# Sample states of a hybrid decoder step: loaded four ahead instead of two, decayed in place by ScalarE, first group one down tile later

## The chip, the cores and the metric

The kernel runs on one core of a Trainium2 chip. The metric is the device time of one execution in microseconds (us), the median of several runs. The engines are TensorE (PE in the profile; PEld is its weight load), VectorE (DVE), ScalarE (ACT), GpSimd (POOL) and SyncE (SP). SP and POOL here mostly issue DMAs; the DMAs of both run on the core's 16 DMA engines.

## The reference, cut to what matters

One inference step of a one-layer decoder, for 512 tokens of a new sequence and 8 sample rows of one token each (520 columns in all): a half-step SwiGLU FFN, a mixer (causal pooling beside a Mamba-2 style SSD), a second half-step FFN, a final norm. The part that the change touches is the new recurrent state of the 8 sample rows, one of the outputs. For a sequence of one token the scan of the reference shrinks to

```
h = a[..., None, None] * h + s      # a = exp(dt * A), s = (dt * x) outer B
```

for 16 heads of 64 x 128 numbers in each of 8 rows. The kernel keeps it as 8 blocks of 128 x 128 for each row: 64 blocks in all. Nothing else reads these new states; they only go to the output. The FFN beside it is

```
def _swiglu(x, wg, wu, wd):
    return (jax.nn.silu(x @ wg) * (x @ wu)) @ wd
```

with a model width of 1024 and an FFN width of 2816, that is 22 feature tiles of 128.

## The kernel before, in words

Every fp32 product is made of three matmuls on a high and a low part: `mm3` (L116 to L119) multiplies high by high (L117), high by low (L118) and low by high (L119). So each weight unit of 128 x 1024 numbers goes through three steps: SP loads it into half of a `raw` pair (a pair holds two units, and there are two pairs), ACT casts it to the high part `whi` (L107), and DVE subtracts that to get the low part `wlo` (L108). There are three buffers for `whi` and three for `wlo`.

An FFN (`class Ffn`) works in chunks of 8, 8 and 6 feature tiles (`rest`, L307). In a chunk it computes gate and up projections (banks `A` and `BE` of PSUM, weights from `w2gu` in the second FFN), and then, in `down` (L339), multiplies the chunk's features `g` with eight down units d = 0 to 7, each 48 matmuls into a bank `dn`. For each d, `done` (L353) takes the bank out: `td` (L356) on DVE, and an add into the residual `h` (L360). `load` (L247) brings in the next gate and up pair; DVE's `s` adds (L258 to L260) read it, and its SP loads (L251, L252) can only start when a `raw` pair is free, that is when DVE has made both low parts of the two down units that sat in it.

The new sample states run inside the second FFN, in the down stages of the first two chunks. `new_states` (L795) is a generator with 16 groups (8 rows by 2 halves); `STATES` (L37) says how many groups are begun ahead of each down unit d, and L376 and L377 advance it. One group is: a load of a broadcast row `br` (64 KB) and of the state `hs` (256 KB), both issued from POOL (L798, L800); four ACT instructions that make an outer product `so` from `br` and the column `sxdt` (L814); four DVE instructions that compute state times decay plus `so` in place (L816); and a store of `hs` from POOL to `out_nss` (L818). The loads of group i + 2 are issued in group i. There are three `br` and three `hs` buffers and two of `so`, so that the load of a new `hs` waits until the store of the group three before it has landed, and POOL's queue stands still behind that wait. The first two groups are loaded long before, when the second FFN begins (L500).

What sets the order: a scheduler orders each engine's instructions by a simulated timeline, apart from those marked to stay in program order among themselves (all of the states' instructions). So a group may end up ahead of or behind a cast, and the order on an engine is fixed when the kernel is built.

Of the kernel before, what the change touches and what calls it, by code (L numbers as in the profile page):

```python
# [9 lines left out]
F32 = mybir.dt.float32  # L10
F32R = mybir.dt.float32r
AF = mybir.ActivationFunctionType
ALU = mybir.AluOpType
# [3 lines left out]
P = 128  # L17
# [16 lines left out]
CHUNKS = (8, 8, 6)  # L34
NG = 9
ON_ACT = 4
STATES = (0, 1, 1, 1, 2, 1, 1, 1)  # L37

CONV_PLAN = (
    "b0 b1 d0 b2 b3 x0 x1 v0 d1 x2 x3 d2 X0 p0 y0 c0 A0 p1 x4 m0 x5 B0 c1 p2 m1 A1 x6 c2 p3 A2 B1 x7 "  # L40
# [22 lines left out]
def tile_trunk_step(ctx: ExitStack, tc: tile.TileContext, ins: dict, outs: dict):  # L63
# [132 lines left out]
    class Ffn:  # L196
# [142 lines left out]
        def down(self, c, lo, hi, after):  # L339
# [35 lines left out]
            for d in range(first, KD):  # L375
                for _ in range(STATES[d] if self.states is not None else 0):  # L376
                    next(self.states)  # L377
# [172 lines left out]
def mixer(tc, ins, outs, e):  # L550
    nc = tc.nc
# [189 lines left out]
    sdec = cst.tile([P, NX, NS], F32, tag="sdec", name="sdec")  # L741
    sxdt = cst.tile([P, NX, NS], F32, tag="sxdt", name="sxdt")
# [5 lines left out]
    def rows_bc(b, a, g):  # L748
        return scr_bc.rearrange("b (a g n) -> b a g n", a=2, g=2)[b, a, g].unsqueeze(0).to_broadcast([P, P])
# [44 lines left out]

    def new_states(wx):  # L795
        def load(b, g):
            br = wx.tile([P, P], F32, tag="sb", bufs=3, name=f"br{b}{g}")
            tc.keep_in_program_order(nc.gpsimd.dma_start(out=br, in_=rows_bc(b, 0, g)))  # L798
            hs = wx.tile([P, 4, P], F32, tag="sh", bufs=3, name=f"hs{b}{g}")
            tc.keep_in_program_order(nc.gpsimd.dma_start(out=hs, in_=ins["state_ssm"][:, b, 4 * g : 4 * g + 4]))  # L800
            return br, hs

        todo = [(b, g) for g in range(2) for b in range(NS)]
        ahead = [load(*todo[0]), load(*todo[1])]
        for i, (b, g) in enumerate(todo):
            yield
            br, hs = ahead.pop(0)
            if i + 2 < len(todo):
                ahead.append(load(*todo[i + 2]))
            o = wx.tile([P, 4, P], F32, tag="so", bufs=2, name=f"so{b}{g}")  # L810
            for q in range(4):
                j = 4 * g + q
                tc.keep_in_program_order(
                    nc.scalar.activation(out=o[:, q], in_=br, func=AF.Copy, scale=sxdt[:, j, b : b + 1]))  # L814
                tc.keep_in_program_order(
                    nc.vector.scalar_tensor_tensor(out=hs[:, q], in0=hs[:, q], scalar=sdec[:, j, b : b + 1],  # L816
                                                   in1=o[:, q], op0=ALU.mult, op1=ALU.add))
            tc.keep_in_program_order(nc.gpsimd.dma_start(out=outs["nss"][:, b, 4 * g : 4 * g + 4], in_=hs))  # L818
        yield

# [268 lines left out]
```

## Time and profile before

| | us |
|---|---|
| time before, median of 3 runs | 1012.86 (1012.05 to 1013.91) |
| the profiled execution, own time | 1014.71 |
| its span | 1012.8 |
| PE busy in the span | 977.1 (96%) |
| DVE, ACT, POOL busy | 807.1, 526.1, 85.9 |
| granted TensorE clock, mean | 0.993 |

The profiled execution lies 1.85 us above the median of the runs, and 1.9 us of its time lie around the span. A line of the timeline or of the windows gives times from the start of the span. In the line of a group or a timeline, the square bracket is the idle time of the engine just before the instruction, and what ended it. The two down stages in question lie at about 730 to 784 us and 860 to 917 us of the span; the first FFN has two down stages of the same work without the states, at 109 to 161 us and 238 to 290 us.

### The profile page before, as it was taken

The numbers are of one execution on the slowest core, as the hardware profiler recorded it, in microseconds if no ns is written. First come the engines' busy times: TensorE is split into PE (matmuls) and PEld (weight loads), VectorE is DVE, ScalarE is ACT, GpSimd is POOL, SyncE is SP. The second block draws the span as 40 slices with busy tenths as digits, with TensorE's granted clock in tenths as the row PEclk, the third lists the DMA queues.
The fourth block names the chain that finished last, engine by engine and source line by source line (L and its number), as shares of the span: only waits on it lengthen the run. The fifth ranks groups of instructions, "written<-read, shape, count | busy, mean of one in ns | idle before, by whom it ended". The sixth has DMA issues, their size and how long they took to land.

```text
span 1012.8 us, 19354 instructions
## 1 busy us (share of the span) xinstructions
PE 977.1 (96%) x7850; PEld 953.8 (94%) x7850; DVE 807.1 (80%) x1408; ACT 526.1 (52%) x877; POOL 85.9 (8%) x157
## 2 busy tenths in 40 slices
PE   7999999999999999999999999999999999999994
PEld 6999999999999999999899989899999999989994
DVE  7999556995569688788979987999847999467866
ACT  7566324664146455685855235666633666434552
POOL 0000000000000000157311000100013000120000
PEclk9999999999999999999999999999999999999997
DMA  6333222332223233363244421332345423453203
GB/s 193 109 125 126 84 84 94 117 105 97 92 84 105 86 105 111 103 200 116 90 144 125 141 84 43 122 126 87 122 137 184 135 108 111 103 188 123 94 32 84
DMA packets 44072, 114.44 MB, mean 113 GB/s; under 512 B 6408, under 2 KB 15560, under 8 KB 43984
## 3 DMA queue, kind: packets, MB, share of 16 engines
q1 hardware_dynamic: 40912, 103.78, 30.0%
q0 software_dynamic: 3072, 9.44, 3.8%
q8 instruction: 61, 1.00, 0.4%
q14 instruction: 27, 0.22, 0.1%
HBM read 105.86 MB, written 7.34 MB: 112 GB/s over the span
## 4 chain that ended last, share of the span: by engine, by line
PE 84%; DVE 8%; ACT 3%; DMA 2%; issue 1%; POOL 0%; SPq 0%; DVEq 0%; ACTq 0%
PE A L117 8%; PE A L118 7%; PE A L119 7%; PE dn L119 6%; PE dn L117 6%; PE BE L117 6%; PE BE L119 6%; PE dn L118 6%; PE BE L118 6%; PE P L230 2%; PE wo L117 2%; PE wo L118 2%; PE wo L119 2%; PE inz L117 2%; DMA raw<-in_w2gu 2%; PE inz L119 2%
## 5 line engine op out<-in xcount | busy, mean ns | idle before, releaser
L117 PE MATMUL dn<-g,whi_1d 128*128 128x260 f32 x352 | 99.5, 283 | 1.8 <-ACT whi_1d L107 1.6
L356 DVE SCALAR_TENSOR_TENSOR td<-dn,r_f 128x520 f32<-128x520 f32 x40 | 27.8, 698 | 90.8 <-PE dn L119 90.8
L118 PE MATMUL dn<-g,whi_1d 128*128 128x260 f32 x352 | 99.4, 283 | 0.0
L119 PE MATMUL dn<-g,wlo_1d 128*128 128x260 f32 x352 | 99.1, 283 | 0.0
L119 PE MATMUL dn<-g,wlo_2d 128*128 128x260 f32 x256 | 73.6, 288 | 3.7 <-DVE wlo_2d L108 3.7
L117 PE MATMUL dn<-g,whi_2d 128*128 128x260 f32 x256 | 73.1, 286 | 0.4 <-ACT whi_2d L107 0.4
L118 PE MATMUL dn<-g,whi_2d 128*128 128x260 f32 x256 | 73.0, 285 | 0.0
L117 PEld LDWEIGHTS dn<-g,whi_1d 128*128 128x128 f32 x352 | 66.2, 188 | 2.4 <-ACT whi_1d L107 2.0
L118 PEld LDWEIGHTS dn<-g,whi_1d 128*128 128x128 f32 x352 | 66.3, 188 | 0.0
L119 PEld LDWEIGHTS dn<-g,wlo_1d 128*128 128x128 f32 x352 | 66.1, 188 | 0.0
L286 ACT COPY ac<-A 128x260 f32<-128x260 f32 x123 | 45.8, 373 | 35.8 <-PE A L119 34.3
L107 ACT CAST whi_1d<-raw_1d 128x1024 fp32r<-128x1024 f32 (+1 forms) x24 | 23.4, 979 | 70.8 <-PE dn L118 62.3
L258 DVE TENSOR_TENSOR s<-raw 128x1024 f32<-128x1024 f32 x41 | 49.9, 1218 | 7.4 <-DMA raw<-in_w2gu 7.4
L119 PEld LDWEIGHTS dn<-g,wlo_2d 128*128 128x128 f32 x256 | 48.9, 191 | 4.6 <-DVE wlo_2d L108 4.6
L230 PE MATMUL P<-xg_f,raw 128*128 128x260 f32 x192 | 45.3, 393 | 5.8 <-DMA raw<-in_w1gu 5.3
L117 PEld LDWEIGHTS dn<-g,whi_2d 128*128 128x128 f32 x256 | 49.1, 192 | 0.6 <-ACT whi_2d L107 0.6
L118 PEld LDWEIGHTS dn<-g,whi_2d 128*128 128x128 f32 x256 | 49.0, 191 | 0.0
L230 PEld LDWEIGHTS P<-xg_f,raw 128*128 128x128 f32 x192 | 37.0, 196 | 11.7 <-ACT xg_f L179 5.3
L118 PE MATMUL wo<-catg,whi_wo 128*128 128x260 f32 x128 | 36.4, 285 | 1.3 <-DVE catg L946 1.3
L117 PE MATMUL wo<-catg,whi_wo 128*128 128x260 f32 x128 | 37.3, 292 | 0.3 <-DVE h L915 0.3
L117 PE MATMUL inz<-xh_mx,whi_inz 128*128 128x260 f32 x128 | 36.8, 287 | 0.0
L117 PE MATMUL inx<-xh_mx,whi_inx 128*128 128x260 f32 x128 | 36.4, 285 | 0.0
(1339 smaller groups left out, 3918.2 us busy)
## 6 DMA issues: line engine op xcount, KB each, us to landing
raw<-in_w2gu SPq DMA_DIRECT2D x44, 512.0 KB, 4.4
raw<-in_w1gu SPq DMA_DIRECT2D x42, 512.0 KB, 4.4
raw_1d<-in_w1d SPq DMA_DIRECT2D x16, 512.0 KB, 4.4
raw_2d<-in_w2d SPq DMA_DIRECT2D x16, 512.0 KB, 4.7
raw_wo<-in_w_out SPq DMA_DIRECT2D x12, 512.0 KB, 4.5
ab<-scr_acs SPq DMA_DIRECT2D x8, 512.0 KB, 4.6
h<-in_state_ssm SPq DMA_DIRECT2D x16, 256.0 KB, 4.4
raw_inz<-in_w_in SPq DMA_DIRECT2D x8, 512.0 KB, 3.9
```

Of the source, the lines that this page charges most:

```text
L107: nc.scalar.copy(h, src)
L117: nc.tensor.matmul(ps, whi, xhi, start=start, stop=False, **kw)
L118: nc.tensor.matmul(ps, whi, xlo, start=False, stop=False, **kw)
L119: nc.tensor.matmul(ps, wlo, xhi, start=False, stop=stop, **kw)
L230: nc.tensor.matmul(self.banks[f, u][b][:, :HB], ws(self.raw[f][:, u], j + 4 * q), xg[:, slot[q]], start=j == q == 0, stop=j == 3 and q == ...
L258: nc.vector.tensor_tensor(out=s1, in0=diag, in1=up0, op=ALU.add)
L286: nc.scalar.copy(keep, out[:, :HB])
L356: nc.vector.scalar_tensor_tensor(out=t, in0=banks[d][:, :, :HB], scalar=-0.5, in1=self.nx[3].rearrange("p (b t) -> p b t", b=2), op0=ALU.mult,
```

## The change

Three things change. Loads: the first four groups are loaded ahead, and group i issues the loads of group i + 4; `br` and `hs` have five buffers each. Arithmetic: ACT now multiplies the state block by its decay in place (the four ACT instructions read and write `hs`), and DVE adds `br` times `sxdt` to it; the tile `so` is gone. Place: in each of the two chunks no group is begun ahead of d = 0 or d = 1, and two groups are begun at d = 3 and at d = 5, where before one was begun at d = 1, 2, 3, 5, 6 and 7 and two at d = 4.

```diff
-STATES = (0, 1, 1, 1, 2, 1, 1, 1)
+STATES = (0, 0, 1, 2, 1, 2, 1, 1)
...
         def load(b, g):
-            br = wx.tile([P, P], F32, tag="sb", bufs=3, name=f"br{b}{g}")
+            br = wx.tile([P, P], F32, tag="sb", bufs=5, name=f"br{b}{g}")
             tc.keep_in_program_order(nc.gpsimd.dma_start(out=br, in_=rows_bc(b, 0, g)))
-            hs = wx.tile([P, 4, P], F32, tag="sh", bufs=3, name=f"hs{b}{g}")
+            hs = wx.tile([P, 4, P], F32, tag="sh", bufs=5, name=f"hs{b}{g}")
             tc.keep_in_program_order(nc.gpsimd.dma_start(out=hs, in_=ins["state_ssm"][:, b, 4 * g : 4 * g + 4]))
             return br, hs
 
         todo = [(b, g) for g in range(2) for b in range(NS)]
-        ahead = [load(*todo[0]), load(*todo[1])]
+        ahead = [load(*t) for t in todo[:4]]
         for i, (b, g) in enumerate(todo):
             yield
             br, hs = ahead.pop(0)
-            if i + 2 < len(todo):
-                ahead.append(load(*todo[i + 2]))
-            o = wx.tile([P, 4, P], F32, tag="so", bufs=2, name=f"so{b}{g}")
+            if i + 4 < len(todo):
+                ahead.append(load(*todo[i + 4]))
             for q in range(4):
                 j = 4 * g + q
                 tc.keep_in_program_order(
-                    nc.scalar.activation(out=o[:, q], in_=br, func=AF.Copy, scale=sxdt[:, j, b : b + 1]))
+                    nc.scalar.activation(out=hs[:, q], in_=hs[:, q], func=AF.Copy, scale=sdec[:, j, b : b + 1]))
                 tc.keep_in_program_order(
-                    nc.vector.scalar_tensor_tensor(out=hs[:, q], in0=hs[:, q], scalar=sdec[:, j, b : b + 1],
-                                                   in1=o[:, q], op0=ALU.mult, op1=ALU.add))
+                    nc.vector.scalar_tensor_tensor(out=hs[:, q], in0=br, scalar=sxdt[:, j, b : b + 1], in1=hs[:, q],
+                                                   op0=ALU.mult, op1=ALU.add))
             tc.keep_in_program_order(nc.gpsimd.dma_start(out=outs["nss"][:, b, 4 * g : 4 * g + 4], in_=hs))
```

## The prediction

> **What bounds the kernel now.** I read the page's first part: PE is busy 96% of the span, so a change to work on ACT, DVE and POOL can only pay where PE stands still for that work. Then the waits of PE in the two down stages of the second FFN, where all the states are computed, then the timelines there, and last the first FFN's down stages, which do the same matmuls without states. The windows view of the four down stages, each from the cast of unit d = 0 to the start of `td` of d = 7 (columns: window, length, busy time of PE, PEld, DVE, ACT, POOL, clock, DMA share, GB/s):
>
> ```profile
> 109.22:161.12 51.90, 50.90 (x423) 50.48 (x422) 23.80 (x29) 10.84 (x13) 0.00 (x0) 1.00 0.27 95
> 237.77:289.92 52.15, 51.15 (x423) 50.73 (x422) 23.79 (x29) 10.84 (x13) 0.00 (x0) 1.00 0.26 93
> 730.12:783.63 53.51, 51.39 (x423) 50.77 (x422) 32.10 (x62) 20.47 (x45) 10.75 (x20) 1.00 0.54 162
> 860.24:916.87 56.63, 53.08 (x423) 52.24 (x422) 32.08 (x62) 20.37 (x45) 9.70 (x18) 0.97 0.50 152
> ```
>
> The states make the stages 53.51 - 51.90 = 1.61 and 56.63 - 52.15 = 4.48 us longer: 6.09 us is the ceiling of what any handling of the states can win. DVE and ACT are not full (32 and 20 of 54 us), so the loss is one of order. PE's timeline at the eighth down unit of both stages shows most of it:
>
> ```profile
> 776.79 0.28 PE L118 MATMUL dn<-g,whi_2d 128*128 128x260 f32 x1
> 777.80 0.39 PE L119 MATMUL dn<-g,wlo_2d 128*128 128x260 f32 x1 [0.73 <-DVE wlo_2d L108]
> ...
> 906.56 0.28 PE L119 MATMUL dn<-g,wlo_2d 128*128 128x260 f32 x1
> 907.25 0.39 PE L117 MATMUL dn<-g,whi_2d 128*128 128x260 f32 x1 [0.41 <-ACT whi_2d L107]
> 907.48 0.28 PE L118 MATMUL dn<-g,whi_2d 128*128 128x260 f32 x1
> 909.52 0.45 PE L119 MATMUL dn<-g,wlo_2d 128*128 128x260 f32 x1 [1.77 <-DVE wlo_2d L108]
> 909.77 0.42 PE L117 MATMUL dn<-g,whi_2d 128*128 128x260 f32 x1
> ```
>
> Matmuls normally start 0.12 us apart. So the first stage loses 777.80 - 776.79 - 0.12 = 0.89 us at d = 7; the second loses 0.57 (cast) and 1.92 (low part), and from 909.77 to 913.02 fifteen matmuls start 0.217 us apart instead of 0.12, another 1.5 us: the granted clock is 0.50 in 911 to 913 us. DVE's timeline says why the low part of d = 7 is late (second stage):
>
> ```profile
> 890.98 2.18 DVE L816 SCALAR_TENSOR_TENSOR hs<-hs,sdec,so 128x128 f32<-128x128 f32 x8
> 893.08 1.22 DVE L108 TENSOR_TENSOR wlo_2d<-raw_2d,whi_2d 128x1024 fp32r<-128x1024 f32 x1
> ...
> 903.52 1.22 DVE L258 TENSOR_TENSOR s<-raw 128x1024 f32<-128x1024 f32 x1 [4.52 <-DMA raw<-in_w2gu]
> 904.78 0.69 DVE L259 TENSOR_TENSOR s<-s,raw 128x512 f32<-128x512 f32 x1
> 905.39 0.69 DVE L356 SCALAR_TENSOR_TENSOR td<-dn,r_f 128x520 f32<-128x520 f32 x1
> 906.00 0.68 DVE L260 TENSOR_TENSOR s<-s,raw 128x512 f32<-128x512 f32 x1
> 906.60 0.69 DVE L360 TENSOR_TENSOR h<-td,h 128x520 f32<-128x520 f32 x1
> 907.21 1.13 DVE L816 SCALAR_TENSOR_TENSOR hs<-hs,sdec,so 128x128 f32<-128x128 f32 x4
> 908.25 1.22 DVE L108 TENSOR_TENSOR wlo_2d<-raw_2d,whi_2d 128x1024 fp32r<-128x1024 f32 x1
> ```
>
> Two groups of states (eight instructions) delay the low part of d = 5. Its end frees the `raw` pair for the next gate and up load, which lands 8.74 us after its second issue (894.69; 7.1 us in the first stage). DVE stands in order before `s`, and behind it lie `s` again, `td`, `s`, `h`, a group of states, and only then the low part that PE waits for.
>
> **The change part by part.** I built the changed kernel and compared the order of instructions on each engine. Outside the two down stages only POOL's early loads move.
>
> Arithmetic: 64 ACT instructions of 388 ns (row L814) and 64 DVE instructions of 344 ns (row L816) are replaced by as many of the same shapes; I take the same durations, bounded by 384 to 405 and 341 to 347 ns, the rows' own extremes: under 1 us of engine time each way, beside PE. ACT no longer waits for a `so` buffer (7.4 us in 4 waits) or for `br` (17.9 us in 6), but now for `hs`.
>
> Loads: two more groups (2 x 320 KB; with the fifth buffer a third too) go out from POOL at about 651 us, 0.54 us of issue each DMA, where POOL has nothing to do until 741. The SP loads of 645 have about landed (4.4 us median) and those of 657 are read at 667.6; cost nothing. If that cover fails, DVE's `s` of the early units waits: at most the time of the extra bytes, 960 KB at the 400 GB/s that the DMA view of 645 to 660 us shows at its peak, 2.4 us; nothing below zero.
>
> Start of the stage: with no group ahead of d = 1, the copy of bank `A` comes 1.3 us earlier on ACT, and PE's order becomes two matmuls of d = 0, the 12 of the next gate unit, the other 46, 12 more, then d = 1: nearly the first FFN's order. There `td` of d = 1 starts 17.70 and 17.75 us after the first cast, here 17.88 (748.00 - 730.12). PE's 0.61 and 0.78 us waits go, and a wait for the low part of d = 1 of about 1.15 us comes: DVE ends it at +11.8 as in the first FFN, while PE has only 12 matmuls to run after +9.0. Gain 0.15 to 0.2 a stage; bounds 0 and 0.25.
>
> Eighth unit: one group, not two, precedes the low part of d = 5, so that load starts 1.05 us earlier (four instructions at a pitch of 0.26). Behind `s` L258, the order is now `td`, `s` L259, low part of d = 7; one `s` (0.6), `h` (0.6) and a group (1.05) move behind it, 2.3 us. Together 3.35 us: the low part is ready for PE at 909.52 - 3.35 = 906.2 and 777.80 - 3.35 = 774.5; PE wants it at about 906.7 and 776.8. Gain 0.89 in the first stage, 2.49 + 1.5 in the second. The margin is 0.5 us in the second stage.
>
> The new cover is on ACT: the cast of d = 7 stands behind the last group's decay, which needs its `hs`. POOL's queue: that load waits for the store of the group five before, and behind it the next store waits. From DVE's times (groups B and C at 755.0 to 757.1) the store of B goes out at 756.1, the next load at about 759, the store of C behind it at about 760, the last load of the stage at 762.7 to 766.3. Such loads took 3.0 to 8.2 us (median 4.5), so 766 to 774.5. Decay (1.28) and cast (1.05) then end at 772 (the cast also waits for the end of d = 5) to 777, and PE wants the cast at 776.7. I take 771.5 for the landing, since the load shares its time with the 1 MB for the next unit, and no stall; bounds 0 and 0.9 a stage. In the second stage no load follows the last group's, so it is easier there.
>
> Here two rules of the Trainium skill bear. Row: the new gate and up pair took 7.1 and 8.7 us to land beside POOL's transfers (DMA share 0.54 and 0.50), and less than 5.3 in the first FFN (issued at 141.14, read at 146.39). DMA: Bandwidth & Descriptors, section Issuing engines are not separate DMA queues, says that DMAs of all issuers run on the same 16 engines and interleave. By that rule loading further ahead moves the bytes but does not take the collision away, so the landing stays at 8.7 us; the sum above holds with that.
>
> Row: 0.89 us of stall left the clock at 1.00, and about 2.8 us with two matmuls in it halved it for 3.5 us. TensorE: Matmul & The Clock Gate, section What's actually happening, has a free-running window of about 3.4 us of idling that halves the clock; by that rule the 1.5 us need not fall in every run, and a rival below counts that.
>
> **Sum.** 0.2 + 0.89 = 1.1 and 0.15 + 2.49 + 1.5 = 4.15: 5.25 us, of the ceiling of 6.09. PE has no slack after it, so it reaches the end: the profiled execution would take 1014.71 - 5.25 = 1009.5. That execution lies 1.85 us above the median; against the median, 1012.86 - 5.25 = 1007.6. About 0.2% (2 us) is what a measurement of this kernel can tell from no change.
>
> **The rivals.**
> - Part of it only. The timed runs may not have the half clock (-1.5 us of gain), or ACT's cast of d = 7 still costs up to 0.9 us a stage: a gain of 3.4 to 3.75, 1009.1 to 1009.4. For it: the median below the profile, and the tight 0.5 us. Against: the chain shortens by more than the stall.
> - No change. The next unit's pair lands 12 us after its second issue in the second stage, because state transfers now fall on it otherwise; then `s` L258, first on DVE, holds the low part of d = 7 until 909.5 as before, half clock included. The first stage alone gains 1.1, the start 0.15: 1011.6. For it: the landing already grew from under 5.3 to 8.7 us beside the states. Against: in the second stage three state loads are left where five were.
> - Slower: decay before the cast. If the last state load of a stage lands more than 13 us after issue (past 778 us), the cast of d = 7 comes past 780, PE idles over 3 us in both stages and loses the clock in both, as in the second stage now: 2 x (56.63 - 52.4) = 8.5 us in place of 5.3, 1012.86 + 3.2 = 1016.1. For it: the ACT instruction now needs 256 KB, not the 64 KB row, and ACT is in order. Against: no state load took over 8.2 us.
>
> **How the numbers follow.** Forecast 0.65, part 0.17, no change 0.08, slower 0.10. Faster by over 0.2% is forecast and part, 0.82. The range starts at the ceiling, 1012.86 - 6.09 = 1006.8, less the 0.8 us by which the fastest run lies under the median, 1006.0; it ends at 1011.0, beyond the part case, with the no change and slower cases left out.
>
> **What would show it.** Right: the two stages about 52.4 us long; no wait of PE for `wlo_2d` at d = 7, one of about 1 us at d = 1; clock 1.00 throughout; ACT's waits for `br` gone. Wrong: `whi_2d` of d = 7 released late behind a decay that waits for `hs`, or `s` L258 waiting 5 us and more for its DMA with PE idle at d = 7.

## The result, and the profile after

The changed kernel took 1010.26 us (median of 14 runs, 1008.5 to 1012.38), the kernel before beside it 1012.28 us (14 runs, 1009.95 to 1013.91): a ratio of 0.9982, 95% interval 0.9974 to 0.9991. That is 2.0 us faster where 5.25 were forecast, and 1010.3 where the prediction said 1007.6. A second measurement on another occasion gave 0.9974 (0.9964 to 0.9985). The sign was right; the size was not.

The profiled execution says otherwise: a span of 1009.0 us and a time of 1011.14 us against 1012.8 and 1014.71, 3.6 us less. Its two down stages of the second FFN, in the windows view (window, length, busy time of PE, PEld, DVE, ACT, POOL, clock, DMA share, GB/s):

```profile
730.77:783.11 52.34, 51.14 (x423) 50.71 (x422) 32.11 (x62) 20.12 (x45) 9.08 (x17) 1.00 0.50 152
859.71:912.22 52.51, 51.31 (x423) 50.72 (x422) 32.11 (x61) 20.13 (x45) 7.51 (x14) 1.00 0.46 147
```

They take 52.34 and 52.51 us, where 52.4 each was forecast, and the clock is 1.00 in both. So within the stages the profiled pair shows the whole forecast gain, 110.14 - 104.85 = 5.29 us. PE's waits in the whole execution of the changed kernel (engine, tile and line, what was waited for: us in total, times, longest):

```profile
...
PE A L117 <- ACT ac L286: 2.7, 6, 1.4
PE dn L119 <- DVE wlo_2d L108: 2.0, 2, 1.0
...
```

The two waits for `wlo_2d` left are those forecast at d = 1 (0.98 us in the first stage), not at d = 7. PE's timeline at the eighth unit of the second stage, where 1.77 us of waiting and the half clock stood before:

```profile
906.04 0.28 PE L117 MATMUL dn<-g,whi_2d 128*128 128x260 f32 x1
906.16 0.28 PE L118 MATMUL dn<-g,whi_2d 128*128 128x260 f32 x1
906.40 0.39 PE L119 MATMUL dn<-g,wlo_2d 128*128 128x260 f32 x1
906.63 0.28 PE L117 MATMUL dn<-g,whi_2d 128*128 128x260 f32 x1
```

906.40 - 906.16 - 0.12 = 0.12 us is all that is left. DVE and ACT in that stage (start, duration, and in brackets the idle time before and what ended it):

```profile
893.36 1.23 DVE L108 TENSOR_TENSOR wlo_2d<-raw_2d,whi_2d 128x1024 fp32r<-128x1024 f32 x1 [1.94 <-ACT whi_2d L107]
...
902.23 1.23 DVE L258 TENSOR_TENSOR s<-raw 128x1024 f32<-128x1024 f32 x1 [2.87 <-DMA raw<-in_w2gu]
903.38 0.69 DVE L356 SCALAR_TENSOR_TENSOR td<-dn,r_f 128x520 f32<-128x520 f32 x1
903.99 0.68 DVE L259 TENSOR_TENSOR s<-s,raw 128x512 f32<-128x512 f32 x1
905.12 1.23 DVE L108 TENSOR_TENSOR wlo_2d<-raw_2d,whi_2d 128x1024 fp32r<-128x1024 f32 x1 [0.45 <-ACT whi_2d L107]
```

```profile
891.11 1.28 ACT L813 ACTIVATE hs<-hs,sdec 128x128 f32<-128x128 f32 x4 [5.81 <-DMA hs<-in_state_ssm]
892.29 1.04 ACT L107 CAST whi_2d<-raw_2d 128x1024 fp32r<-128x1024 f32 x1
...
902.86 1.29 ACT L813 ACTIVATE hs<-hs,sdec 128x128 f32<-128x128 f32 x4 [5.61 <-DMA hs<-in_state_ssm]
904.05 1.03 ACT L107 CAST whi_2d<-raw_2d 128x1024 fp32r<-128x1024 f32 x1
```

Two things are to be seen. The low part of d = 7 now stands third behind `s` L258, and what it waits for is ACT: a decay that waits for `hs` and then the cast. And the low part of d = 5 waits 1.94 us for its own cast, which stands behind another such decay; so the SP load of the next pair is issued at 894.62, not 1.05 us earlier than before (894.32).

So the open question is the difference between the profiled pair (3.6 us, 5.3 less in the stages, 1.5 more around them) and the timed runs (2.0 to 2.6). The 1.5 us more arise because the first profile took only 1012.8 - 110.14 = 902.66 us outside the two stages, where the later profiles of both kernels took 903.4 to 904.5.

### The profile page after: what moved, and what is told of

It reads as the page before. It is cut to its first block, busy times and chain, and to the rows that moved or that the text cites. A ratio compares the mean times of both kernels' runs of the same rounds, so it can differ in the third digit from the quotient of the medians.

```text
span 1009.0 us, 19357 instructions
## 1 busy us (share of the span) xinstructions
PE 976.1 (97%) x7850; PEld 952.9 (94%) x7850; DVE 807.6 (80%) x1408; ACT 525.3 (52%) x877; POOL 85.7 (8%) x157
## 4 chain that ended last, share of the span: by engine, by line
PE 91%; DVE 4%; ACT 2%; issue 1%; POOL 0%; DMA 0%; SPq 0%; DVEq 0%; ACTq 0%
PE A L117 8%; PE A L118 7%; PE A L119 7%; PE dn L119 7%; PE dn L117 7%; PE dn L118 7%; PE BE L117 6%; PE BE L119 6%; PE BE L118 6%; PE P L230 4%; PE wo L117 2%; PE wo L118 2%; PE wo L119 2%; PE inz L117 2%; PE inz L119 2%; PE inz L118 2%
## 5 line engine op out<-in xcount | busy, mean ns | idle before, releaser
L258 DVE TENSOR_TENSOR s<-raw 128x1024 f32<-128x1024 f32 x41 | 50.0, 1220 | 4.5 <-DMA raw<-in_w2gu 4.5
```

Of the source, the lines that this page charges most:

```text
L258: nc.vector.tensor_tensor(out=s1, in0=diag, in1=up0, op=ALU.add)
```

## The experiments

Theory: what is lost in these stages is what the late gate and up pair costs through the order of DVE, and that the pair lands as late as in the one profile is an accident of that execution. Rivals: the arithmetic of the states itself costs the time; the transfers themselves do; or the order was not what brought the gain. All ratios below are to runs of the kernel before on the same chip. "Landing" is counted from the pair's first SP issue to the start of `s` L258; the prediction and the expectations count from the second issue, 0.37 us later (about 0.95 in `e13` and `e14`).

**The kernel before, again, and without its states.** `e1` is the kernel before, unchanged. `e2` and `e6` are one kernel, run twice, that leaves out all but one of the 16 groups of states:

```diff
-        ahead = [load(*todo[0]), load(*todo[1])]
+        ahead = [load(*todo[0])] * 16
...
-            if i + 2 < len(todo):
-                ahead.append(load(*todo[i + 2]))
+            if i:
+                continue
```

> The kernel before, unchanged, profiled a second time. Stage 1 and stage 2 are the two down stages of the second FFN, from the first whi_2d cast to td of d = 7 (53.51 and 56.63 us in the first profile, 52.34 and 52.51 after the change; two predicted, 52.4 each). The stages gained 5.29 us in the profiles but the medians only 2.0. Theory U (the profiled execution of before was an unlucky one): stage 2 is now 53 to 55 us, the clock stays at 1.00 in it, and the pair for the next unit lands in under 8 us. Rival G (given back): stage 2 is 56.6 us again with half a clock at d = 7, and the 3 us that are missing lie outside the two stages in the changed kernel.

> Leaves out 15 of the 16 state groups (their loads, arithmetic and stores), so the new sample states are not computed but for one group. It measures the ceiling in timed runs. Theory U: 2.2 to 3.5 us faster than before, only some 0.8 us faster than the change. Rival G: about 6 us faster than before, since the stages of before always cost 6.1 us more than the first FFN's. Stage 2 in its profile: 52.2 us by both.

> Leaves out 15 of the 16 state groups, as e2, timed beside the change on one chip: the ceiling. Theory V: 3 to 4 us faster than before, under 1 us faster than the change. Rival G: 1.5 to 2 us faster than the change.

`e1`, a single run of 1018.5 us, had stages of 56.34 and 56.31 us, each with the half clock: my expectation of 53 to 55 us fell. `e2` had 52.31 and 52.05 and took 0.9963 of before (0.9948 to 0.9977), `e6` 52.33 and 52.06, and 0.9969 (0.9959 to 0.9978): 3.1 to 3.8 us. That is what the handling of 15 of the 16 groups costs in the timed runs, not the 6 us that the rival of `e2` gave; the ceiling of 6.09 us in the prediction was that of one execution. `e6` ran beside a second measurement of the change:

> The changed kernel, unchanged, beside before and two others on one chip. New theory V: the wait at d = 7 in the kernel before varies between executions by several us (stages of 53.5, 56.6, 56.3 and 56.3 us in two profiles); the change takes it away wholly (stages 52.3 and 52.5), and the two profiled executions of before lay on the slow side. Then the change is 2 to 4 us faster than before here too, its runs keep a mean clock of 0.994 to 0.995 where about half of the runs of before show 0.993 or less, and the change lies within 1 us of the kernel without states. Rival G (given back outside the stages): it lies 1.5 to 2 us above the kernel without states, with stages of 52.5 us in its profile.

The change took 1011.1 us (0.9974; 0.9964 to 0.9985), the kernel without states 1010.91. Little is left to win here.

**One part of the change at a time.** `e3` has the new `STATES` line alone. `e4` has the loads and the arithmetic of the change with the old `STATES`. `e11` has the arithmetic alone, and `e12` loads three ahead with the old arithmetic:

```diff
 e3:  -STATES = (0, 1, 1, 1, 2, 1, 1, 1)
      +STATES = (0, 0, 1, 2, 1, 2, 1, 1)
...
 e12: -            br = wx.tile([P, P], F32, tag="sb", bufs=3, name=f"br{b}{g}")
      +            br = wx.tile([P, P], F32, tag="sb", bufs=4, name=f"br{b}{g}")
...
      -        ahead = [load(*todo[0]), load(*todo[1])]
      +        ahead = [load(*t) for t in todo[:3]]
...
```

> Only the places of the groups are changed; loads two ahead and the arithmetic as before. By the prediction's steps the order (one group, not two, ahead of the low part of d = 5; the low part of d = 7 right behind the first s adds) carries the gain, and the loads nothing: as fast as the change, within 0.5 us, stages near 52.4 to 53.0; one group now stands on DVE ahead of s L258, which may cost up to 1 us at d = 7. Rival (loads carry it): within 0.5 us of before, with ACT waiting for br ahead of the cast of d = 7.

> Loads four ahead and decay in place, but the groups where they were. By the prediction's steps: same DVE order as before, so the low part of d = 7 is as late as before; within 0.5 us of before, stage 1 near 53.5, stage 2 as in before. Rival (loads carry it): as fast as the change.

> The kernel before with the in-place arithmetic alone (decay on ACT, outer product added by DVE), loads two ahead, old places. Theory (loading further ahead carries the gain): as before or slower, 0.999 to 1.003, since ACT's first instruction of a group now waits for 256 KB that were issued two groups ago, and the casts stand behind it; stages of 53 to 57 us. Rival (the in-place arithmetic carries it, since no so buffer is waited for): 0.997 to 0.999, stages below 53 us.

> The kernel before with its arithmetic and places, but loads three ahead and four buffers of br and hs (four ahead does not fit beside the so tiles). Theory (loading further ahead carries the gain): 0.997 to 0.999, ACT's waits for br below 5 us in sum (before 17.9), stages of 52.4 to 53.5 us. Rival (only together with the in-place arithmetic): 0.9993 to 1.001.

| | ratio | interval | stages in the profile, us |
|---|---|---|---|
| `e3` place alone | 1.002 | 1.0008 to 1.0033 | 55.15, 56.67 |
| `e4` loads and arithmetic | 0.9982 | 0.9971 to 0.9992 | 52.85, 52.42 |
| `e11` arithmetic alone | 0.9995 | 0.9981 to 1.001 | 52.90, 52.65 |
| `e12` loads three ahead | 0.9996 | 0.9982 to 1.001 | 53.45, 56.17 |

My expectations for `e3` and `e4` fell: the new place alone is slower, and the rest of the change gains without it. ACT of `e3`, second stage, and the waits of ACT and PE in its whole execution:

```profile
901.07 1.28 ACT L814 ACTIVATE so<-br,sxdt 128x128 f32<-128x128 f32 x4 [7.14 <-DMA br<-scr_bc]
902.25 1.03 ACT L107 CAST whi_2d<-raw_2d 128x1024 fp32r<-128x1024 f32 x1
```

```profile
ACT so L814 <- DMA br<-scr_bc: 25.3, 8, 7.1
...
PE dn L117 <- ACT whi_2d L107: 1.9, 2, 1.6
```

With loads two ahead, two groups begun together at d = 5 need a row that has not come; the cast of d = 6 stands behind them on ACT, and PE waits for it. (The 55.15 us of its first stage hold no wait of PE at d = 7: there `td` itself is late on DVE, behind a group that waits for `hs`.) So the place alone does harm while the loads are two ahead and the arithmetic is the old one. `e4`, without the place, gained as much as the whole change in its timed runs. Against my expectation it does not keep the old order: in its second stage the low part of d = 7 stands ahead of `h` and of the group, 3.08 us behind `s` L258:

```profile
899.84 1.23 DVE L258 TENSOR_TENSOR s<-raw 128x1024 f32<-128x1024 f32 x1 [0.66 <-DMA raw<-in_w2gu]
...
902.92 1.22 DVE L108 TENSOR_TENSOR wlo_2d<-raw_2d,whi_2d 128x1024 fp32r<-128x1024 f32 x1
```

In its first stage that distance is the old one, 4.74 us. `e11` met the time expected of it, but its stages are as short as its rival said (its profiled execution took 905.4 us outside them, so they do not tell its time). `e12` met the time of its rival: its stages did not come below 53.4 us, and ACT still waited 7.1 us for `br`. Neither is told from no change, nor, with intervals this wide, from each other; which of loads and arithmetic does the work in `e4` stays open.

**Is it the transfers or the arithmetic?** `e9` keeps the order on DVE and all arithmetic, but hardly any transfer; `e10` keeps the transfers, but hardly any arithmetic:

```diff
 e9:
-            br, hs = ahead.pop(0)
-            if i + 2 < len(todo):
-                ahead.append(load(*todo[i + 2]))
+            br, hs = ahead[i % 2]
...
-            tc.keep_in_program_order(nc.gpsimd.dma_start(out=outs["nss"][:, b, 4 * g : 4 * g + 4], in_=hs))
+            if i >= 14:
+                tc.keep_in_program_order(nc.gpsimd.dma_start(out=outs["nss"][:, b, 4 * g : 4 * g + 4], in_=hs))
 e10:
-            for q in range(4):
+            for q in range(1):
...
-                    nc.scalar.activation(out=o[:, q], in_=br, func=AF.Copy, scale=sxdt[:, j, b : b + 1]))
+                    nc.scalar.activation(out=o[:, q, :8], in_=br[:, :8], func=AF.Copy, scale=sxdt[:, j, b : b + 1]))
...
-                    nc.vector.scalar_tensor_tensor(out=hs[:, q], in0=hs[:, q], scalar=sdec[:, j, b : b + 1],
-                                                   in1=o[:, q], op0=ALU.mult, op1=ALU.add))
+                    nc.vector.scalar_tensor_tensor(out=hs[:, q, :8], in0=hs[:, q, :8], scalar=sdec[:, j, b : b + 1],
+                                                   in1=o[:, q, :8], op0=ALU.mult, op1=ALU.add))
```

> The kernel before with its orders and its arithmetic, but the state loads for the first two groups alone and the stores for the last two alone (the other loads and stores of the states are left out, so most new states are not written). Theory (the states' DMA traffic makes the gate and up pair land late, and that lateness is the loss at the eighth down unit): the pair lands within 5.5 us, both down stages take 52.3 to 52.9 us, and the time is within 0.1% of the kernel without states, 0.996 to 0.998 of before. Rival (the queue of state arithmetic on DVE and ACT is the loss by itself): stages of 53 to 56 us, 0.9995 to 1.000.

> The converse: all loads and stores of the states as before, but of each group only one of four ACT and one of four DVE instructions, on 8 of 128 columns (the rest of the state arithmetic is left out). Theory (the transfers' lateness costs only as far as DVE's and ACT's state work stands behind it): the pair still lands in 6.5 to 8.8 us, but the low part of the eighth unit comes some 2 us earlier, so stages of 52.2 to 52.8 us and 0.996 to 0.998. Rival (traffic alone is enough): PE still waits 0.5 us and more at d = 7, stages of 53 us and more, 0.9985 to 1.000.

`e9` took 0.9972 (0.996 to 0.9983), `e10` 0.9973 (0.996 to 0.9986): neither is told from the kernel without states. Their stages, `e9` and then `e10`:

```profile
730.90:783.41 52.51, 51.12 (x423) 50.71 (x422) 32.25 (x61) 20.46 (x45) 0.00 (x0) 1.00 0.28 94
860.02:912.41 52.39, 51.01 (x423) 50.59 (x422) 32.28 (x61) 20.48 (x45) 1.09 (x2) 1.00 0.31 104
```

```profile
730.05:782.74 52.69, 51.49 (x423) 50.81 (x422) 24.81 (x37) 12.74 (x21) 10.75 (x20) 1.00 0.55 165
859.34:911.60 52.26, 51.15 (x423) 50.68 (x422) 24.90 (x37) 12.75 (x21) 9.70 (x18) 1.00 0.54 166
```

DVE's 32 us of work without transfers cost nothing that these runs can tell, and neither does a DMA share of 0.55 without the state work on DVE. So the loss needs both: transfers that make the pair late, and state work on DVE. Where on DVE, `e10` does not separate. Its pair goes out 2.0 us earlier than in the kernel before, 32.12 us after the stage's first cast in place of 34.1, since no group delays the low part of d = 5; behind `s` L258 only 0.7 us are gone (4.07 in place of 4.74). Both expectations held in stages and time; the first landing of `e10`, 9.02 us from the second issue, lies above the 8.8 expected.

**How late, and what it costs.** The profiled executions of the kernel before differ in the landing. `e7` and `e15` are two more profiles of it, `e16` one more of the change (`e1` and `e14` to `e16` are single runs, used for their stages alone):

> The kernel before once more: a null measurement and a third profile. Ratio to before 1.000 within 0.1%. Theory V: its stages lie anywhere between 52.5 and 57 us, and the sum of both stages tells the span: span less stages 903.6 within 1.5 us, as in the other five profiles (902.5 to 905.4).

> The kernel before, one look more. Theory (the landing sets the stage length): each stage on the line 52.4 at 5.0, 52.9 at 6.5, 53.5 at 7.1, 56.3 at 8.5 us, within 0.4 us. Rival (something else differs between executions): off that line by 1 us and more.

> The changed kernel, one look more. Theory: landings of 6.5 to 8 us and stages of 52.3 to 53.2 us. Rival (its landing is as variable as the old kernel's 5.0 to 8.8 us): a landing over 8 us in a stage, then 53.4 us and more.

`e7`, run in full beside `e5`, took 0.9999 (0.9986 to 1.0013), a measure of the noise. Its expectation held. In the second stage of its profile the pair lands 2.4 us sooner than in the profile that the prediction used:

```profile
901.16 1.23 DVE L258 TENSOR_TENSOR s<-raw 128x1024 f32<-128x1024 f32 x1 [2.14 <-DMA raw<-in_w2gu]
...
905.90 1.22 DVE L108 TENSOR_TENSOR wlo_2d<-raw_2d,whi_2d 128x1024 fp32r<-128x1024 f32 x1
```

```profile
730.80:783.65 52.85, 51.39 (x423) 50.76 (x422) 32.12 (x61) 20.47 (x45) 10.71 (x20) 1.00 0.55 166
860.26:912.98 52.72, 51.28 (x423) 50.66 (x422) 32.10 (x61) 20.47 (x45) 9.66 (x18) 1.00 0.55 164
```

To see the changed order with a late pair too, `e13` and `e14` put a copy between the two loads of the pair, in the changed kernel, whose order of instructions on PE, DVE, ACT and POOL stays as it was:

```diff
+            if i == 2 and f in (10, 18):
+                extra = dr.tile([P, 1024], F32, name=f"extra_{n}")
+                tc.keep_in_program_order(nc.sync.dma_start(out=raw[:, 0], in_=src[2 * f]))
+                tc.keep_in_program_order(nc.sync.dma_start(out=extra, in_=src[2 * f - 2]))
+                tc.keep_in_program_order(nc.sync.dma_start(out=raw[:, 1], in_=src[2 * f + 1]))
...
```

In `e14` the copy has 512 columns in place of 1024.

> The changed kernel with an additional copy of 512 KB from a weight to scratch memory between the two loads of the gate and up pair of the down stages (f = 10 and 18), so that the pair lands later. Theory (the changed order hides about 7.2 us of landing and then loses one for one): landing of 8.2 to 9.0 us, stages of 53.4 to 54.3 us, clock 1.00, so 2 to 3.5 us in all over the changed kernel and about 0.9995 to 1.001 of before; at such a landing the old order took 56.3 to 56.6 us a stage, so the forecast gain would be there. Rival (the new order fails like the old one once the pair is late): stages above 55.5 us, with half clock, 1.002 and more.

> As the last, with an additional copy of 256 KB. Theory: landing of 7.6 to 8.3 us, stages of 52.8 to 53.6 us. Rival: above 54 us.

`e13` took 0.9987 (0.997 to 1.0005): with the pair delayed in both stages, it is still not slower than the kernel before. The stages of both orders in one table, in us; the last two columns, the start of the low part of d = 7 and the stage's length, count from the first cast of the stage:

| stage | landing | `s` to low part | low part | length |
|---|---|---|---|---|
| before, first and second | 7.54, 9.20 | 4.74, 4.73 | 46.41, 48.01 | 53.51, 56.63 |
| `e1` | 8.86, 8.87 | 4.74, 4.74 | 47.70, 47.70 | 56.34, 56.31 |
| `e7` | 6.89, 6.82 | 4.74, 4.74 | 45.74, 45.64 | 52.85, 52.72 |
| `e15` | 6.61, 9.09 | 4.73, 4.75 | 45.45, 47.90 | 52.55, 54.99 |
| `e12` (before's order) | 7.48, 8.73 | 4.74, 4.74 | 46.34, 47.55 | 53.45, 56.17 |
| after | 7.64, 7.61 | 2.89, 2.89 | 44.17, 45.41 | 52.34, 52.51 |
| `e5` (the change) | 7.46, 8.03 | 2.89, 2.89 | 43.98, 45.92 | 52.35, 53.04 |
| `e16` (the change) | 7.02, 8.29 | 2.88, 2.89 | 43.34, 45.86 | 52.35, 52.97 |
| `e14` (256 KB more) | 8.59, 8.34 | 2.43, 2.49 | 44.40, 45.31 | 52.31, 52.42 |
| `e13` (512 KB more) | 9.70, 9.95 | 2.35, 2.35 | 45.59, 47.40 | 52.69, 54.52 |

One rule fits both orders: a stage takes the start of that low part plus 7.1 us, and never less than about 52.3; four stages of the old order (the second of before, both of `e1`, the second of `e12`) are 1.5 us longer still, with the half clock. Both stages of `e11` and the first of `e4` follow the rule too. The old order passes the landing on plus 4.74 us, the new one plus 2.89 or less. My expectations for `e13` and `e14` held only in part: `e14` came out below its range (52.31 and 52.42), `e13` just outside on both sides (52.69 and 54.52), its time below the 0.9995 to 1.001 expected, though the interval reaches into it. At these landings the changed order loses less than the old one does. `e16` met its range. `e15` met its line in the first stage and missed it in the second (54.99 us at a landing of 8.72 from the second issue, where the line has 56.3 at 8.5): PE waited as long as elsewhere, but the clock stayed. The matmuls behind that wait, `e12` above, `e15` below:

```profile
909.22 0.58 PE L119 MATMUL dn<-g,wlo_2d 128*128 128x260 f32 x1 [1.98 <-DVE wlo_2d L108]
909.60 0.42 PE L117 MATMUL dn<-g,whi_2d 128*128 128x260 f32 x1
909.81 0.42 PE L118 MATMUL dn<-g,whi_2d 128*128 128x260 f32 x1
```

```profile
908.11 0.39 PE L119 MATMUL dn<-g,wlo_2d 128*128 128x260 f32 x1 [1.76 <-DVE wlo_2d L108]
908.34 0.28 PE L117 MATMUL dn<-g,whi_2d 128*128 128x260 f32 x1
908.46 0.28 PE L118 MATMUL dn<-g,whi_2d 128*128 128x260 f32 x1
```

**A version meant to be better.** `e8` is the changed kernel with other places, none at d = 4 and d = 6:

```diff
-STATES = (0, 0, 1, 2, 1, 2, 1, 1)
+STATES = (0, 1, 2, 2, 0, 1, 0, 2)
```

> The change with other places, (0, 1, 2, 2, 0, 1, 0, 2): no group on DVE between the two takeouts that lead to the low part of d = 5, none ahead of the low part of d = 7, and the groups that need late loads behind the cast of d = 6. If the length of DVE's chain from the low part of d = 5 to that of d = 7 still costs anything in the changed kernel, this is up to 1 us faster than the change; by theory V the change has no wait left at d = 7 and this is the same within 0.5 us. If late state loads ahead of the cast of d = 7 are what is left, this loses 1 us and more at d = 7 again.

It took 1.0021 (1.0008 to 1.0033), with stages of 53.68 and 55.08: slower, where I had expected a gain, no change or a loss at d = 7. ACT's timeline and PE's wait in the whole execution say why:

```profile
740.12 2.44 ACT L813 ACTIVATE hs<-hs,sdec 128x128 f32<-128x128 f32 x8
742.47 0.35 ACT L286 COPY ac<-A 128x260 f32<-128x260 f32 x1
```

```profile
PE A L117 <- ACT ac L286: 6.2, 6, 1.9
```

Eight decays in a row stand ahead of the copy of bank `A`, and the next gate unit's matmuls wait for that copy: 6.2 us in all, 2.7 in the change, and of these 1.9 in each of the two stages, 0.2 in the change. `td` of d = 1 starts 19.04 and 20.56 us after the first cast, 17.70 and 17.72 in the change. So the groups moved forward from d = 4, 5 and 6 to d = 1 and 2 cost more there than they could save later.

## Why the prediction was wrong in size

- **What bounds, and where.** Right. The loss sat at the low part of d = 7, PE lost it one for one, and it ended with the change. The forecast stage length of 52.4 us came out as 52.34 and 52.51, in the second stage with luck, as the fourth point says.
- **The term that failed: "0.89 in the first stage, 2.49 + 1.5 in the second".** It was read from one execution and treated as a property of the kernel. Over the eight stages of the kernel before that were profiled, the landing runs from 6.61 to 9.20 us and the length from 52.55 to 56.63, 54.49 in the mean, 108.98 for a pair of stages against 110.14 in the one used. The six stages of the change average 52.59. The timed runs put the whole cost of the states at 3.1 to 3.8 us, not 6.09, and the gain at 2.0 to 2.6. The prediction set this execution 1.85 us above the median and still subtracted its full loss from the median. A smaller gain was listed as a rival ("Part of it only", 1009.1 to 1009.4), but that one took only the half clock and the cast into account, not a sooner landing, and still gave a larger gain (3.4 to 3.75) than was measured. Even the means of the profiles leave 108.98 - 2 x 52.59 = 3.8 us of gain in the stages, 1.2 to 1.8 more than the timed runs show. How often the pair lands late in a timed run can't be read, since those runs leave no trace: that sooner landings make up the rest is not shown. The mean granted clock that each timed run has on record fits, and settles nothing: of the 105 runs of the kernel before that were timed beside the experiments, 46 show 0.993 or less and took 1014.6 us in the mean, 32 show 0.995 and took 1012.5; but 4 of the 12 runs of the change in `e5` and 3 of the 11 of `e6`, with hardly any states, show 0.993 as well, which `e5` had not expected.
- **"That load starts 1.05 us earlier."** Not so. It was issued 33.64 us into the first stage instead of 34.13, 0.5 us earlier, but 34.91 instead of 34.08 in the second, 0.8 later, because the cast of d = 5 stands behind a decay that waits 5.81 us for `hs`. The prediction weighed that wait only for the cast of d = 7.
- **"2.3 us move behind it."** DVE's order gives this: 4.74 - 2.35 = 2.39 us in `e13`. But in the plain runs ACT's decay and cast end later than DVE's order allows, and it is 4.74 - 2.89 = 1.85. By 34.91 + 9.20 + 2.89 = 47.0 and the rule of the table, the second stage would have taken about 54.1 us at the landing of the profile used, an estimate: 2.5 us better than 56.63, not 4.1. The claimed margin of 0.5 us was not there; that the stage took 52.51 us all the same was luck: the landing was shorter, 7.61 us.
- **The cast of d = 7 behind the last decay.** The bounds of 0 and 0.9 held, and "no stall" in four of the six stages of the change; two lost 0.6 to 0.7 us (53.04 and 52.97, against 52.35). Both are second stages, where the prediction said it was easier. ACT's waits for `br` are gone, as forecast, but it now waits 25.0 us for `hs`, as long as it waited for `br` and the `so` buffers before (17.9 + 7.4). In none of the six did the state load come late enough for the rival "decay before the cast".
- **The start of the stage.** Right: `td` of d = 1 starts 748.47 - 730.77 = 17.70 us after the first cast, 17.88 before.
- **The order carries the gain, the loads cost nothing and bring nothing.** Wrong as a division. The place alone loses 2 us (`e3`), and loads with arithmetic gain as much without it (`e4`), where they shorten the order of the second stage by themselves. How much of the gain is the order's and how much the landing's stays open there.
- **The clock.** By TensorE: Matmul & The Clock Gate (section What's actually happening) of the Trainium skill, the window is free-running, so that the half clock need not follow each stall. The runs agree: of the five stages of the old order in which the low part started past 47.5 us, with waits of 1.76 to 1.98 us at the same place, four lost the clock and the second of `e15` kept it at 1.00. They do not agree with the idle window of about 3.4 us that the prediction took from there: a single wait of 1.76 us (both stages of `e1`) was enough.
- **Landing stays where it is.** By DMA: Bandwidth & Descriptors (section Issuing engines are not separate DMA queues) of the Trainium skill, DMAs of all issuers run on the same 16 engines and interleave, so that loading further ahead should not take the collision away. The traces agree: 7.68 us in the mean of the change's six stages, 7.99 in before's eight, against 4.8 and 4.9 where `e9` has hardly any state transfers. But the prediction's 8.7 us was one execution's: counted as there, the change's mean is 7.3.

## What to carry to other kernels

A stall that ends with a DMA's landing should be sized from several profiled executions, or from a run without the suspected work, before it is put into a sum; if the one profile is slower than the median, that can be a sign that its stall is larger than usual. Read a chain as "landing plus so many us of the order behind it": the two parts vary separately, and an order that puts the work PE waits for directly behind the late instruction leaves more room for a late landing. Where a wait moves from one engine to another, follow every cast behind it, those that start the next load too.

## What the runs showed that was not expected

- The same 1 MB load, at the same place of the same kernel, landed 6.6 to 9.2 us after its issue beside the state transfers; in `e15` 6.61 in the one stage and 9.09 in the other.
- In all six stages of the changed kernel the last group's decay began 0.62 to 0.63 us after `s` L258, whether the pair landed after 7.0 or after 8.3 us: the last state load, issued on POOL's queue 1.3 to 1.6 us after the pair (895.93 and 894.62 in the second stage of the first profile), ended almost with it. So in these stages DVE's `s` and the decay ahead of ACT's cast became ready together, at every landing seen.
- The half clock cost 1.5 us each time (matmuls 0.217 us apart in place of 0.12), and whether it came behind nearly equal waits differed between executions (`e12` and `e15`).
